# The channel mixer's depthwise taps read the gate from PSUM, and VectorE takes nearly all low parts of its weights

## The chip, the cores and the metric

The kernel runs on one core of one Trainium2 chip. The metric is the device time of one execution in microseconds (us). Ratios compare medians of runs taken side by side.

## The reference, cut to what matters

One layer of a diffusion backbone over 512 latent tokens of width 1024. After two token mixers comes the channel mixer, which is the part that is changed: a GEGLU network whose gate passes through a 3x3 depthwise convolution over the latent grid of 8 rows by 64 columns, with zeros outside the grid.

```python
def _conv_ffn(h, w_up, cw, cb, w_down, grid_h, grid_w):
    up = h @ w_up                                     # 1024 -> 2 x 2816
    g = _dwconv2d(up[..., :D_FF].reshape(B, grid_h, grid_w, D_FF), cw, cb).reshape(B, T, D_FF)
    return (jax.nn.gelu(g) * up[..., D_FF:]) @ w_down  # 2816 -> 1024
```

All of it is float32.

## The kernel before

**Products.** Every large product is made of three passes on TensorE. Each operand is split into a high part (`wh`, a cast) and a low part (`wl`, the operand less its high part), and `mm3` adds high x high, high x low and low x high in one PSUM bank. `Weights.prepare` (lines 85 to 97) makes the weights' parts block by block: a load into `raw` (two buffers), a cast to `wh` on ScalarE (line 93) and a subtraction to `wl` on VectorE or, for blocks marked `on_pool`, on GpSimd (line 95). `wh` and `wl` have three buffers each, so a block waits for the product three blocks earlier. `W.take` prepares two blocks ahead, with a raised priority.

**The channel mixer.** The 2816 gate channels and 2816 value channels are 22 tiles of 128 channels, in two stages: tiles 0 to 11, then 12 to 21. For each tile TensorE makes the gate `pg` and the value `pv`, one weight block and 24 matmuls of 512 columns each, into two of the six PSUM banks of the pool `ps`. Then `up_post` (lines 789 to 807) works on the tile: ScalarE copies the gate to a padded SBUF grid `gpad` (line 792, three buffers) and makes the centre tap with the bias in `acc` (line 794, two buffers); VectorE adds the eight other taps, each a multiply-add over a shifted window of the padded copy (line 797); ScalarE applies the GELU (line 800); VectorE multiplies with `pv` (line 802); ScalarE and VectorE split the result into `fh` and `fl` (lines 805, 806). After the tiles of a stage come its down products (`d`), in two halves with four PSUM tiles each. Tiles 0 and 1 are made with the halves of the second norm, and tiles 2 to 5 are each followed by the transposes of `token_major`.

**Order.** Each engine runs its instructions in an order that the tile planner fixes beforehand, from priorities and its own estimate of when each is ready. PSUM banks are handed out by the planner as well: a bank is free when the last reader of its tile is done. In the kernel before, the low parts of tile 0 and of all odd tiles are on GpSimd, the others on VectorE. The blocks of `w_down` are all on VectorE.

Of the kernel before, what the change touches and what calls it, by code (L numbers as in the profile page):

```python
# [10 lines left out]
F32 = mybir.dt.float32  # L11
F32R = mybir.dt.float32r
AF = mybir.ActivationFunctionType
ALU = mybir.AluOpType
PSUM = bass.MemoryType.PSUM

P = 128
# [11 lines left out]
GRID_W = 64  # L29
ROWS = T // GRID_W  # L30
# [77 lines left out]
def hybrid_block(ctx: ExitStack, tc: tile.TileContext, a: dict, out: bass.AP):  # L108
    nc = tc.nc

    def pool(name, bufs=1, side="left"):
        return tc.tile_pool(name=name, bufs=bufs, side=side, reuse_waits="tile")

    def opened(name, bufs=1, side="left"):
        stack = ExitStack()
        return stack, stack.enter_context(pool(name, bufs, side))
# [30 lines left out]
    def add_tiles(name, j, n=BLK, **kw):  # L147
        W.add(a[name][j], [n, n], **kw)
# [21 lines left out]
        add_tiles("w_out", i)  # L170
    for i0, i1 in STAGES:
        for i in range(i0, i1):
            add_tiles("w_up", i, on_pool=i == 0 or i % 2 == 1, extra=i == 0)
        for hf in range(2):
            for i in range(i0 // 2, i1 // 2):
                W.add(a["w_down"][hf, i], [BLK])
# [3 lines left out]
    def col(name, i, n=1):  # L180
        o = _cols[name] + i
        return sm[:, o : o + n]
# [190 lines left out]
    with pool("lamp") as lp:  # L373
# [3 lines left out]
        q = lp.tile([P, 20], F32, name="q")  # L377
# [21 lines left out]
    for i in range(2):  # L399
        t = lru.tile([P, PADW], F32, name=f"pad{i}")  # L400
# [199 lines left out]
    with pool("sp") as sp:  # L600
# [4 lines left out]
        for j in range(NG):  # L605
# [9 lines left out]
            for n in range(4):  # L615
                nc.vector.scalar_tensor_tensor(s[:, n, :], pz[:, n * P : (n + 1) * P], col("gv", j), bsb[:, j, :],
                                               op0=ALU.mult, op1=ALU.add)
# [158 lines left out]
            nc.scalar.copy(x1[:, t, hf * T : (hf + 1) * T], tp)  # L776


    GP = GRID_W + 2
    fp, f_pool = opened("f", side="right")  # L780
    fw = ctx.enter_context(pool("ffn"))
    gpads = []
    for i in range(3):
        t = fw.tile([P, ROWS + 2, GP], F32, name=f"gpad{i}")
        nc.gpsimd.memset(t, 0.0)
        gpads.append(t)
    fs = {}

    def up_post(i, pg, pv):
        pad = gpads[i % 3]  # L790
        g3 = pg.rearrange("p (r c) -> p r c", c=GRID_W)
        nc.scalar.copy(pad[:, 1 : 1 + ROWS, 1 : 1 + GRID_W], g3)
        acc = fw.tile([P, ROWS, GRID_W], F32, tag="acc", name=f"acc{i}", bufs=2)
        nc.scalar.activation(acc, g3, AF.Identity, scale=col("ffw", 9 * i + 4), bias=col("ffb", i))  # L794
        for q in (0, 1, 2, 3, 5, 6, 7, 8):
            dy, dx = q // 3, q % 3
            nc.vector.scalar_tensor_tensor(acc, pad[:, dy : dy + ROWS, dx : dx + GRID_W], col("ffw", 9 * i + q),  # L797
                                           acc, op0=ALU.mult, op1=ALU.add)
        accf = acc.rearrange("p r c -> p (r c)")
        nc.scalar.activation(accf, accf, AF.Gelu_apprx_tanh)  # L800
        f = fw.tile([P, T], F32, tag="f", name=f"f{i}", bufs=2)
        nc.vector.tensor_tensor(f, accf, pv, op=ALU.mult)
        fh = f_pool.tile([P, T], F32R, tag="fh", name=f"fh{i}", bufs=14)
        fl = f_pool.tile([P, T], F32R, tag="fl", name=f"fl{i}", bufs=14)
        nc.scalar.copy(fh, f)
        nc.vector.tensor_tensor(fl, f, fh.bitcast(F32), op=ALU.subtract)
        fs[i] = (fh, fl)
# [8 lines left out]
    for st, (i0, i1) in enumerate(STAGES):  # L816
        i = i0
        if st == 0:
            up_post(0, pu[0, 0], pu[0, 1])
            up_post(1, pu[1, 0], pu[1, 1])  # L820
            i = 2
        while i < i1:
            for s in range(2):
                pu[i, s] = mm_tile(f"up{i}{s}")
                gemm(pu[i, s], W.take(), h2h, h2l)
            up_post(i, pu[i, 0], pu[i, 1])
            if 2 <= i < 6:
                token_major(i - 2)
            i += 1
# [103 lines left out]
```

## Time and profile before

| What | Value |
|---|---|
| median of 3 runs (lowest to highest) | 991.13 us (991.07 to 996.96) |
| the profiled execution's own time | 989.86 us |
| its span, first to last instruction | 988.1 us |
| mean granted TensorE clock | 0.995 of full speed |
| PE (TensorE matmul) busy | 951.6 us |
| DVE (VectorE) busy | 665.2 us (67%) |
| ACT (ScalarE) busy | 478.0 us (48%) |
| POOL (GpSimd) busy | 95.0 us (10%) |
| chain that ended last | PE 65%, DVE 16%, ACT 8%, issue 6% |

Matmuls overlap their neighbours in the records, so the busy time of PE is longer than the time its stream needs; the distance between the starts of matmuls is the better measure. The channel mixer fills the span from about 604 us on.

### The profile page before, as it was taken

Reading aid. Unit: us, or ns where it says so; the run is one execution under the profiler, and the core shown is the slowest. Engines: PE = TensorE matmul, PEld = TensorE weight load, DVE = VectorE, ACT = ScalarE, POOL = GpSimd, SP = SyncE. Lnnn points to the kernel's source line nnn. Section 1 sums busy time; section 2 is a strip of 40 time slices with the busy share of each in tenths; the row PEclk is TensorE's granted clock in tenths of the full one; section 3 lists DMA queues with packets and bytes.
Section 4 is the critical chain, followed back from the end, with each engine's and each line's share of the span. In section 5 each row is a group of like instructions: output and inputs, shape, how many; then the busy total and the mean of one; then the engine's idle time right before and its main releaser. Section 6 shows DMA issues by size and latency. Waiting matters only on the chain.

```text
span 988.1 us, 11916 instructions
## 1 busy us (share of the span) xinstructions
PE 951.6 (96%) x4787; PEld 789.4 (80%) x4787; DVE 665.2 (67%) x867; ACT 478.0 (48%) x661; POOL 95.0 (10%) x92
## 2 busy tenths in 40 slices
PE   3999999999999999999999998999999999999997
PEld 2788888888888788788888798888778888887686
DVE  3768496968574976586634456798886447888764
ACT  4546979786989552234222343443333213333333
POOL 0000000000000011100001031222220002222020
PEclk9999999999999999999999999999999999999999
DMA  9532212132222276734524331222213332221232
GB/s 355 223 134 86 78 51 86 43 107 86 86 86 86 86 257 233 257 148 175 198 97 170 111 125 43 86 86 86 85 43 108 105 128 86 85 86 64 84 109 86
DMA packets 23511, 116.85 MB, mean 118 GB/s; under 512 B 2576, under 2 KB 3744, under 8 KB 14368
## 3 DMA queue, kind: packets, MB, share of 16 engines
q1 hardware_dynamic: 17488, 94.59, 26.9%
q0 software_dynamic: 5968, 21.50, 6.2%
q8 instruction: 37, 0.61, 0.2%
q14 instruction: 18, 0.15, 0.1%
HBM read 113.98 MB, written 2.10 MB: 117 GB/s over the span
## 4 chain that ended last, share of the span: by engine, by line
PE 65%; DVE 16%; ACT 8%; issue 6%; DMA 3%; POOL 1%; SPq 0%; ACTq 0%; DVEq 0%; POOLq 0%
DVE acc L797 8%; PE d L140 4%; PE d L141 4%; PE d L139 4%; PE up L139 4%; PE up L141 4%; PE up L140 4%; DVE wl L95 2%; DMA wmod<-in_w_mod 2%; ACT wh L93 2%; PE pg L139 2%; PE pg L140 2%; PE pg L141 2%; PE gg L141 1%; PE gg L140 1%
## 5 line engine op out<-in xcount | busy, mean ns | idle before, releaser
L93 ACT CAST wh<-raw 128x1024 fp32r<-128x1024 f32 (+1 forms) x156 | 161.3, 1038 | 231.6 <-PE d L141 44.6
L95 DVE TENSOR_TENSOR wl<-raw,wh 128x1024 fp32r<-128x1024 f32 (+1 forms) x132 | 159.4, 1210 | 119.9 <-ACT wh L93 119.3
L797 DVE SCALAR_TENSOR_TENSOR acc<-gpad,sm,acc 128x512 f32<-128x512 f32 x176 | 159.4, 916 | 19.1 <-ACT acc L794 15.0
L141 PE MATMUL up<-h2h,wl 128*128 128x512 f32 (+1 forms) x384 | 145.1, 378 | 6.8 <-POOL wl L95 6.8
L139 PE MATMUL up<-h2h,wh 128*128 128x512 f32 (+1 forms) x384 | 144.8, 377 | 1.4 <-ACT wh L93 1.4
L140 PE MATMUL up<-h2l,wh 128*128 128x512 f32 (+1 forms) x384 | 143.9, 375 | 0.0
L141 PEld LDWEIGHTS up<-h2h,wl 128*128 128x128 f32 x384 | 73.2, 191 | 23.3 <-POOL wl L95 8.8
L95 POOL TENSOR_TENSOR wl<-raw,wh 128x1024 fp32r<-128x1024 f32 x24 | 61.2, 2552 | 292.4 <-ACT wh L93 280.4
L139 PEld LDWEIGHTS up<-h2h,wh 128*128 128x128 f32 x384 | 73.1, 190 | 14.8 <-ACT wh L93 2.9
L140 PEld LDWEIGHTS up<-h2l,wh 128*128 128x128 f32 x384 | 73.3, 191 | 12.5
L800 ACT ACTIVATE acc<-acc 128x512 f32<-128x512 f32 x22 | 13.9, 632 | 134.5 <-DVE acc L797 134.5
L140 PE MATMUL d<-wl,fh 128*128 128x512 f32 (+1 forms) x186 | 72.0, 387 | 0.1
L141 PE MATMUL d<-wh,fl 128*128 128x512 f32 (+1 forms) x186 | 71.1, 382 | 0.0
L139 PE MATMUL d<-wh,fh 128*128 128x512 f32 (+1 forms) x186 | 71.0, 382 | 0.0
L558 DVE SCALAR_TENSOR_TENSOR wmod<-wmod,cbx 128x1024 f32<-128x1024 f32 x24 | 29.2, 1222 | 27.4 <-DMA wmod<-in_w_mod 27.3
L140 PEld LDWEIGHTS d<-wl,fh 128*128 128x128 f32 x186 | 34.9, 188 | 8.8 <-DVE wl L95 1.4
L139 PEld LDWEIGHTS d<-wh,fh 128*128 128x128 f32 x186 | 34.9, 188 | 7.9
L141 PEld LDWEIGHTS d<-wh,fl 128*128 128x128 f32 x186 | 35.0, 188 | 7.2
L555 POOL DMA_DIRECT2D wmod<-in_w_mod x32 | 16.9, 528 | 246.4 <-DVE yrl L538 128.8
L474 DVE TENSOR_TENSOR i<-i,xr 128x768 f32<-128x768 f32 x20 | 18.9, 954 | 19.7 <-ACT i L467 19.7
L140 PE MATMUL pr<-yrl,wh 128*128 128x512 f32 x80 | 31.7, 396 | 0.0
L141 PE MATMUL pr<-yrh,wl 128*128 128x512 f32 x80 | 31.7, 396 | 0.0
(316 smaller groups left out, 2162.1 us busy)
## 6 DMA issues: line engine op xcount, KB each, us to landing
raw<-in_w_up SPq DMA_DIRECT2D x22, 1024.0 KB, 4.7
wmod<-in_w_mod POOLq DMA_DIRECT2D x32, 512.0 KB, 4.1
raw<-in_w_down SPq DMA_DIRECT2D x22, 512.0 KB, 3.2
wm<-in_w_mod SPq DMA_DIRECT2D x8, 1024.0 KB, 8.8
raw<-in_w_lru SPq DMA_DIRECT2D x5, 1024.0 KB, 4.7
raw<-in_w_pr SPq DMA_DIRECT2D x5, 1024.0 KB, 6.4
raw<-in_w_rx SPq DMA_DIRECT2D x4, 1024.0 KB, 4.8
raw<-in_w_rg SPq DMA_DIRECT2D x4, 1024.0 KB, 4.7
```

Of the source, the lines that this page charges most:

```text
L93: nc.scalar.copy(h[:, :n], r)
L95: eng.tensor_tensor(l[:, :n], r, h[:, :n].bitcast(F32), op=ALU.subtract)
L139: nc.tensor.matmul(o, wh, xh, start=first, stop=False)
L140: nc.tensor.matmul(o, wh, xl, start=False, stop=False)
L141: nc.tensor.matmul(o, wl, xh, start=False, stop=last)
L474: nc.vector.tensor_tensor(i[u], i[u], xr[h][:, u % 2, :], op=ALU.mult)
L555: nc.gpsimd.dma_start(wm, a["w_mod25"][n - 2, k])
L558: nc.vector.scalar_tensor_tensor(wm, wm, 1.0, cbx, op0=ALU.mult, op1=ALU.mult, accum_out=m)
L797: nc.vector.scalar_tensor_tensor(acc, pad[:, dy : dy + ROWS, dx : dx + GRID_W], col("ffw", 9 * i + q), acc, op0=ALU.mult, op1=ALU.add)
L800: nc.scalar.activation(accf, accf, AF.Gelu_apprx_tanh)
```

## The change

The taps read the gate where TensorE left it, in PSUM. Each tap covers only the part of the grid for which its shifted source exists: 7 of 8 rows when it reaches up or down, 63 of 64 columns when it reaches left or right. The padded copies, their memsets and the ScalarE copy are removed. The low parts of `w_up` are all on VectorE, except those of tiles 0 and 1, which stay on GpSimd.

```diff
-            add_tiles("w_up", i, on_pool=i == 0 or i % 2 == 1, extra=i == 0)
+            add_tiles("w_up", i, on_pool=i <= 1, extra=i == 0)
...
-    gpads = []
-    for i in range(3):
-        t = fw.tile([P, ROWS + 2, GP], F32, name=f"gpad{i}")
-        nc.gpsimd.memset(t, 0.0)
-        gpads.append(t)
...
-        pad = gpads[i % 3]
         g3 = pg.rearrange("p (r c) -> p r c", c=GRID_W)
-        nc.scalar.copy(pad[:, 1 : 1 + ROWS, 1 : 1 + GRID_W], g3)
         acc = fw.tile([P, ROWS, GRID_W], F32, tag="acc", name=f"acc{i}", bufs=2)
         nc.scalar.activation(acc, g3, AF.Identity, scale=col("ffw", 9 * i + 4), bias=col("ffb", i))
         for q in (0, 1, 2, 3, 5, 6, 7, 8):
-            dy, dx = q // 3, q % 3
-            nc.vector.scalar_tensor_tensor(acc, pad[:, dy : dy + ROWS, dx : dx + GRID_W], col("ffw", 9 * i + q),
-                                           acc, op0=ALU.mult, op1=ALU.add)
+            dy, dx = q // 3 - 1, q % 3 - 1
+            r0, r1 = max(0, -dy), ROWS - max(0, dy)
+            c0, c1 = max(0, -dx), GRID_W - max(0, dx)
+            o = acc[:, r0:r1, c0:c1]
+            nc.vector.scalar_tensor_tensor(o, g3[:, r0 + dy : r1 + dy, c0 + dx : c1 + dx], col("ffw", 9 * i + q), o,
+                                           op0=ALU.mult, op1=ALU.add)
```

## Rows read from the trace of the kernel before

**Rows 1.** The page, part 1: busy time, share of the span, instructions.
```profile
PE 951.6 (96%) x4787; PEld 789.4 (80%) x4787; DVE 665.2 (67%) x867; ACT 478.0 (48%) x661; POOL 95.0 (10%) x92
```
**Rows 2.** Waits of PE in the up products: total us, times, longest.
```profile
PE up L141 <- POOL wl L95: 6.8, 4, 1.7
...
PE up L139 <- ACT wh L93: 1.4, 3, 0.5
```
**Rows 3.** Windows: length, busy (count) per engine, granted clock, DMA share, GB/s.
```profile
622.00:686.00 64.00, 64.00 (x302) 53.37 (x301) 56.65 (x66) 32.09 (x47) 15.33 (x6) 1.00 0.24 82
686.00:734.00 48.00, 45.36 (x194) 35.35 (x193) 39.15 (x44) 15.33 (x22) 8.42 (x5) 1.00 0.23 77
734.00:743.00 9.00, 7.30 (x24) 5.52 (x25) 7.83 (x9) 1.86 (x3) 2.20 (x1) 0.81 0.22 64
743.00:812.00 69.00, 69.00 (x297) 55.53 (x296) 34.03 (x42) 18.00 (x20) 0.40 (x1) 1.00 0.35 122
812.00:890.00 78.00, 78.00 (x345) 64.61 (x345) 62.01 (x66) 25.63 (x35) 17.49 (x7) 1.00 0.24 81
890.00:924.00 34.00, 30.13 (x128) 23.34 (x128) 26.81 (x31) 12.26 (x17) 7.52 (x3) 1.00 0.18 62
924.00:946.00 22.00, 21.90 (x93) 16.79 (x92) 15.51 (x19) 8.25 (x11) 0.00 (x0) 1.00 0.34 103
```
**Rows 4.** Timeline of DVE, end of stage one: start us, us, what.
```profile
722.50 8.28 DVE L797 SCALAR_TENSOR_TENSOR acc<-gpad,sm,acc 128x512 f32<-128x512 f32 x8
...
734.96 5.72 DVE L797 SCALAR_TENSOR_TENSOR acc<-gpad,sm,acc 128x512 f32<-128x512 f32 x6 [1.42 <-ACT acc L794]
...
746.30 1.23 DVE L95 TENSOR_TENSOR wl<-raw,wh 128x1024 fp32r<-128x1024 f32 x1 [0.26 <-ACT wh L93]
747.46 4.69 DVE L797 SCALAR_TENSOR_TENSOR acc<-gpad,sm,acc 128x512 f32<-128x512 f32 x6
752.06 1.22 DVE L95 TENSOR_TENSOR wl<-raw,wh 128x1024 fp32r<-128x1024 f32 x1
753.20 1.53 DVE L797 SCALAR_TENSOR_TENSOR acc<-gpad,sm,acc 128x512 f32<-128x512 f32 x2
```
**Rows 5.** Timeline of ACT, the same stretch.
```profile
743.30 0.63 ACT L800 ACTIVATE acc<-acc 128x512 f32<-128x512 f32 x1 [7.44 <-DVE acc L797]
...
745.22 1.05 ACT L93 CAST wh<-raw 128x1024 fp32r<-128x1024 f32 x1
746.17 0.58 ACT L792 COPY gpad<-up 128x512 f32<-128x512 f32 x1
746.64 0.78 ACT L794 ACTIVATE acc<-up,sm 128x512 f32<-128x512 f32 x1
...
754.77 0.63 ACT L800 ACTIVATE acc<-acc 128x512 f32<-128x512 f32 x1 [6.41 <-DVE acc L797]
```
**Rows 6.** The line of the taps: shortest, median, longest ns, first and last start.
```profile
L797 DVE SCALAR_TENSOR_TENSOR acc<-gpad,sm,acc x176: 736/752/2896, 625.4 to 936.9; 128x512 f32<-128x512 f32 x176
```
**Rows 7.** Lines by form: xcount, busy us, mean ns, idle before, releaser.
```profile
L797 DVE SCALAR_TENSOR_TENSOR acc<-gpad,sm,acc 128x512 f32<-128x512 f32 x176 | 159.4, 916 | 19.1 <-ACT acc L794 15.0
...
L673 DVE SCALAR_TENSOR_TENSOR x1c<-o,mcol,x1c 128x512 f32<-128x512 f32 x5 | 3.8, 751 | 14.7 <-PE o L141 14.7
L673 DVE SCALAR_TENSOR_TENSOR x1c<-o,mcol,x1c 128x256 f32<-128x256 f32 x6 | 2.9, 476 | 2.3 <-PE o L141 2.3
```
**Rows 8.** The page, part 6: weight loads, KB each, us to landing.
```profile
raw<-in_w_up SPq DMA_DIRECT2D x22, 1024.0 KB, 4.7
```
**Rows 9.** Timelines of DVE, PE and ACT at the first tiles.
```profile
625.39 12.74 DVE L797 SCALAR_TENSOR_TENSOR acc<-gpad,sm,acc 128x512 f32<-128x512 f32 x14 [0.96 <-ACT acc L794]
...
634.05 0.48 PE L139 MATMUL up<-h2h,wh 128*128 128x512 f32 x1
...
638.16 0.63 ACT L800 ACTIVATE acc<-acc 128x512 f32<-128x512 f32 x1 [1.61 <-DVE acc L797]
```

More of the change, by code (lines that the diff above doesn't have):

```diff
@@ L776, in token_major @@
             nc.scalar.copy(x1[:, t, hf * T : (hf + 1) * T], tp)
-    GP = GRID_W + 2
     fp, f_pool = opened("f", side="right")
     fw = ctx.enter_context(pool("ffn"))
-    gpads = []
-    for i in range(3):
-        t = fw.tile([P, ROWS + 2, GP], F32, name=f"gpad{i}")
-        nc.gpsimd.memset(t, 0.0)
-        gpads.append(t)
     fs = {}
     def up_post(i, pg, pv):
-        pad = gpads[i % 3]
         g3 = pg.rearrange("p (r c) -> p r c", c=GRID_W)
-        nc.scalar.copy(pad[:, 1 : 1 + ROWS, 1 : 1 + GRID_W], g3)
         acc = fw.tile([P, ROWS, GRID_W], F32, tag="acc", name=f"acc{i}", bufs=2)
```

## The prediction

> **What bounds the kernel now.** I began with the busy times on the page: PE is busy for 96% of the span [rows 1], which says that only what shortens PE's stream or its gaps can shorten the run. The list of PE's waits names 8.2 us in the up products, most of it for low parts from GpSimd [rows 2]. That is too little, since overlapping matmuls hide the start of a gap, so I counted matmuls per window instead [rows 3]. From 812 to 890 us PE starts 345 in 78 us, 0.226 us apart; that is its pace when nothing is late, and a tile (48 matmuls) then takes 10.85 us. At that pace the other windows of the up products need 194 x 0.226 = 43.9 of 48 us, 24 x 0.226 = 5.4 of 9, and 128 x 0.226 = 28.9 of 34: 4.1, 3.6 and 5.1 us are lost. The down products run 0.232 apart (297 in 69 us), so 924 to 946 loses 22 - 93 x 0.232 = 0.4. The sum is **13.2 us**. Part of the 3.6 is TensorE at the lower of its levels for a while: the window's granted clock is 0.81, after PE had waited.
>
> Why only there? The timelines show that the work behind the products goes round in a loop, one turn per tile: GELU, product with the value, `fh`, next `wh`, its `wl`, taps, GELU. The taps of three tiles running start at 722.50, 734.96 and 747.46 [rows 4], 12.5 us apart, which is 1.65 more than PE's 10.85. So PE's lead over that loop shrinks by 1.65 us per tile. In stage two it lasts from 812 to 890 us, 7 tiles, or some 11.6 us of lead; then PE waits for weight parts at each turn.
>
> **The loop without GpSimd** is already in the trace. Behind the last tile of each stage come blocks of `w_down`, whose low parts are all VectorE's. The GELUs at 743.30 and 754.77 enclose such a turn: 11.47 us [rows 5], although VectorE makes two low parts in it [rows 4]. The six taps from 747.46 take 4.69 us there, but 5.72 from 734.96, when GpSimd works, and eight take 8.28 from 722.50. The line's median tap is 752 ns, its longest 2896 [rows 6], its mean 916 [rows 7]: taps that meet GpSimd wait for it. That is 176 x 0.164 = 28.9 us of VectorE, against 20 x 1.14 us (752.06 to 753.20) = 22.8 us for the 20 low parts that are moved.
>
> **The change, part by part.**
>
> *Low parts moved.* The loop becomes the one of 11.47 us for every tile: 1.0 us less. Behind a low part that waits for `wh` stand the taps on VectorE, and behind those the GELU; the 11.47 includes both. GpSimd's queue loses work and nobody else waits for it. The raw buffer of an odd tile comes free later, as its second low part now stands behind six taps; the load lands in 4.7 us [rows 8] and has more than a turn, so nothing.
>
> *Smaller taps.* Four corners of 7 x 63, two of 7 x 64, two of 8 x 63: 458.5 elements on average, not 512. The nearest row with a PSUM source is the same operation at line 673: 751 ns for 512 elements and 476 for 256 [rows 7], 1.07 ns per element. So a tap is 752 - 53.5 x 1.07 = 695 ns, 0.46 us less per tile: a loop of **11.0 us**. Bounds: 476 ns below, 916 above (a tap as slow as today's mean). I take 695, since line 673 reads PSUM while PE writes other banks and is no slower than a padded tap.
>
> [...]
>
> *The copy removed.* It takes 0.5 us of ScalarE at 746.17, but `acc` ends at 747.42 and `wl` at 747.53 [rows 4, 5]: the low part releases the taps just as late. Nothing inside the loop; about 0.5 us at a stage's first taps. The memsets sit on an idle GpSimd: nothing.
>
> *PE's lead.* 11.0 against 10.85 costs 0.15 us of lead per tile, 1.5 per stage, out of 11.6. The lead is no longer used up, and of the 13.2 us lost I take all back but 0.2. If the lower clock of 734 to 743 came from elsewhere, up to 1.6 us of it would stay (the 9 us at 0.81 are worth 7.3 at full clock).
>
> *Banks held longer.* The gate's bank came free after `acc`; now it is held to the last tap. In the regular part this costs nothing: tile i+3 takes tile i's banks 32.6 us after tile i began, and the taps are done by then. At the first tiles it does. Tiles 0, 1 and 2 fill all six banks, and tile 3 begins at 634.05 [rows 9]. Taps of tiles 0 and 1 are interleaved: 14 run from 625.39, and the GELU of tile 0 waits for the last of them, until 638.16 [rows 9]. Afterwards, 14 x 0.71 (with the gap between two) = 9.9 us, and one of tile 3's low parts among them 1.1 (the other fits where the copies were): bank free at 636.5, so PE waits **2.5 us**, and no later slack takes it back. Bounds: 0, if tile 0's taps all go first (625.4 + 5.7 + 1.1 = 632.2), and 5.0, if all 16 taps and both low parts do (639.1).
>
> **Sum.** 989.9 - 13.2 + 0.2 + 2.5 = 979.4 on the profiled execution's own time (989.86, 1.8 above its span). The median of the runs is 991.13, 1.3 higher: **980.5 us** to the half. Its own range is 976 to 984: no wait for a bank below (978), a wait of 5.0 and a leftover clock dip above.
>
> **Rivals.**
>
> *The waits only change hands* (0.20). Every odd tile's second low part goes behind six taps, where GpSimd made it at once. If the planner puts it later, behind all eight, or orders the weight casts anew, PE waits for VectorE instead. For it: orders are fixed beforehand and will be made anew. Against it: even tiles have had this order all along, and the 812 to 890 window, which holds such tiles, loses nothing. It leaves about the 8.2 us of recorded waits in place: 980.5 + 8.2, so 985 to 990.
>
> *Taps from PSUM cost more* (0.08). The lead of 11.6 us over 10 tiles allows a loop of 12.0, so taps up to 0.695 + 1.0 / 8 = 0.82 us; beyond that each further 0.1 us per tap costs 0.8 us per late tile. At 916 ns the loop is 12.8 and all is lost: 982 to 992. For it speaks only that no row has eight reads of one bank in a row, in pieces of rows; against it, line 673 [rows 7]. [...]
>
> *Banks starve PE all through* (0.12), the slower side. If taps of two tiles are interleaved not only at the start but all through stage one, each pair holds both gates to the end, and PE waits at each of six pairs for up to the 5.0 us above: 989.9 - 13.2 + 30 = 1006.7, so 1002 to 1008 on the median. It decides when a tile's last tap comes over 32.6 us after its gate's first product. For it: the banks are just enough for three tiles. Against it: in the regular part six and two, or eight, taps of one tile follow each other [rows 4].
>
> **Chances.** My forecast has 0.60, the rivals 0.20, 0.08 and 0.12. The range of 8 in 10 is 976 to 990: the forecast, the first rival and most of the second. About 1% (9.9 us, to 981.2) is what a measurement here can tell from no change, and the forecast lies just beyond it: of its 0.60, some 0.10 falls short. So faster 0.50, same 0.10 + 0.20 + 0.08 = 0.38, slower 0.12.
>
> **What would show it.** The GELUs of a stage should stand 10.9 to 11.1 us apart, not 12.5. Taps should take 0.67 to 0.75 us, with none above 1 us once tile 1's low parts are made. PE should start its up products 0.226 to 0.23 us apart through both stages, with no wait at line 141 for a low part. It should wait once, near 634 us, for a VectorE tap. Taps of 0.8 us and more, a chain of waits for `wl` on VectorE, or a wait for banks at every second tile would prove me wrong, each for its rival. The down products and the tail should take as long as before.

## The result, and the profile after

The changed kernel takes **977.5 us** (median of 4 runs, 975.9 to 979.2). The kernel before, run beside it on the same chip, takes 993.0 (4 runs, 991.1 to 997.0). The ratio is 0.985, with an interval of 0.983 to 0.988: 1.5% faster. The profiled execution of the changed kernel took 978.6 us with a span of 976.8; before it was 989.9 and 988.1.

The first lines to read are the busy times and the shares of the chain that ended last, from the page of the changed kernel.

```profile
PE 947.4 (97%) x4787; PEld 790.9 (81%) x4787; DVE 645.4 (66%) x887; ACT 469.6 (48%) x639; POOL 41.6 (4%) x69
...
PE 78%; issue 6%; DVE 6%; ACT 6%; DMA 3%; POOL 1%; SPq 0%; POOLq 0%; DVEq 0%; ACTq 0%
```

The chain ran through PE for 65% of the span and through DVE for 16%; now it is 78% and 6%. PE's busy time hardly moves (951.6 to 947.4), although the span is 11 us shorter. Busy time counts an instruction from its start to its modelled end, so a busy PE can hide late starts. DVE makes 20 more instructions than before and is busy 20 us less [rows 1].

Counting the matmuls says more. These are windows of the changed kernel: length, then busy time and count per engine (PE, PEld, DVE, ACT, POOL), then granted clock, DMA share and GB/s.

```profile
622.00:686.00 64.00, 64.00 (x313) 53.87 (x312) 55.87 (x78) 29.20 (x40) 0.00 (x0) 1.00 0.28 99
686.00:734.00 48.00, 48.00 (x213) 39.75 (x213) 39.39 (x53) 18.11 (x24) 0.00 (x0) 1.00 0.23 77
734.00:743.00 9.00, 9.00 (x41) 7.33 (x40) 8.00 (x12) 2.19 (x3) 0.00 (x0) 1.00 0.36 117
812.00:890.00 78.00, 78.00 (x346) 64.58 (x345) 65.02 (x86) 27.68 (x36) 0.00 (x0) 1.00 0.27 95
890.00:924.00 34.00, 34.00 (x150) 27.94 (x149) 26.84 (x36) 11.14 (x14) 0.00 (x0) 1.00 0.27 87
...
625.30:737.70 112.40, 112.40 (x514) 93.39 (x513) 98.75 (x135) 46.91 (x63) 0.00 (x0) 1.00 0.27 94
804.90:913.80 108.90, 108.90 (x482) 90.10 (x482) 88.74 (x117) 38.27 (x49) 0.00 (x0) 1.00 0.26 91
913.79:969.88 56.09, 56.09 (x271) 46.51 (x269) 28.41 (x42) 19.15 (x33) 6.32 (x4) 1.00 0.22 76
```

Set the first five against [rows 3]. In 686 to 734 PE starts 213 matmuls where it started 194; 890 to 924 has 150 for 128. The pace of 812 to 890, 0.226 us per matmul, now holds in the other windows of up products too (48 / 213 and 34 / 150 are 0.225 and 0.227), and the granted clock is 1.00 in all of them. The last three windows are the up products of the two stages and the last down products, by their own beginnings and ends. The same stretches of the kernel before, which begin and end elsewhere in time, are these three.

```profile
622.35:743.00 120.65, 116.31 (x514) 93.90 (x513) 103.62 (x118) 49.06 (x71) 25.95 (x10) 0.99 0.23 79
810.20:924.30 114.10, 110.23 (x481) 89.65 (x480) 90.70 (x98) 38.95 (x53) 25.41 (x10) 1.00 0.22 78
924.31:981.15 56.84, 56.74 (x271) 46.18 (x269) 35.80 (x51) 22.31 (x38) 6.45 (x4) 1.00 0.28 93
```

The up products of stage one take 112.4 us instead of 120.65 (514 matmuls in both), those of stage two 108.9 instead of 114.1, and the last down products 56.1 instead of 56.8: **8.25 + 5.2 + 0.75 = 14.2 us** taken back. The down products of stage one take 67.2 in both (737.7 to 804.9 now, 743.0 to 810.2 before). The span fell by 11.3 only, since the work ahead of these stages ended 2.9 us later in this execution (the first product of tile 2 starts at 625.26, before at 622.35). That is not the change: a transfer of `wmod` came late there (VectorE waits 3.88 us for it, until 429.86). In the same kernel profiled again the point is 622.40, and over all ten profiled executions of the experiments below it lies anywhere from 622.4 to 626.0.

Where the taps stand is seen in their line, all 176 of them (shortest, median, longest ns), and in the groups by form, which end in mean ns and the idle time ahead.

```profile
L793 DVE SCALAR_TENSOR_TENSOR acc<-up,sm,acc x176: 662/677/744, 625.2 to 917.4; 128x441 f32<-128x441 f32 x88, 128x448 f32<-128x448 f32 x44, 128x504 f32<-128x504 f32 x44
```
```profile
L793 DVE SCALAR_TENSOR_TENSOR acc<-up,sm,acc 128x441 f32<-128x441 f32 x88 | 58.7, 672 | 12.1 <-ACT acc L786 10.7
...
L793 DVE SCALAR_TENSOR_TENSOR acc<-up,sm,acc 128x504 f32<-128x504 f32 x44 | 32.6, 740 | 1.2
...
L793 DVE SCALAR_TENSOR_TENSOR acc<-up,sm,acc 128x448 f32<-128x448 f32 x44 | 30.0, 682 | 1.2
```

No tap waits any more: the longest takes 744 ns, where it was 2896 [rows 6], and the mean is 121.3 us / 176 = 689 instead of 916 [rows 7].

ScalarE's timeline near the end of stage one shows who leads now (start, duration, what, and the idle time ahead with what ended it).

```profile
698.61 0.63 ACT L796 ACTIVATE acc<-acc 128x512 f32<-128x512 f32 x1 [3.37 <-DVE acc L793]
...
705.07 1.05 ACT L93 CAST wh<-raw 128x1024 fp32r<-128x1024 f32 x1 [3.19 <-PE up L140]
709.49 0.63 ACT L796 ACTIVATE acc<-acc 128x512 f32<-128x512 f32 x1 [3.37 <-DVE acc L793]
```

The GELUs stand 10.88 us apart, and the casts between them wait for PE to free a `wh`. The turn is now as long as PE's 48 matmuls; the loop follows PE, no longer PE the loop. In PE's list of waits no up product appears.

### The profile page after: what moved, and what is told of

Same layout as the page of the kernel before. It is cut to its first block, busy times and chain, and to the rows that moved or that the text cites. A ratio compares the mean times of both kernels' runs of the same rounds, so it can differ in the third digit from the quotient of the medians.

```text
span 976.8 us, 11886 instructions
## 1 busy us (share of the span) xinstructions
PE 947.4 (97%) x4787; PEld 790.9 (81%) x4787; DVE 645.4 (66%) x887; ACT 469.6 (48%) x639; POOL 41.6 (4%) x69
## 4 chain that ended last, share of the span: by engine, by line
PE 78%; issue 6%; DVE 6%; ACT 6%; DMA 3%; POOL 1%; SPq 0%; POOLq 0%; DVEq 0%; ACTq 0%
PE up L139 8%; PE up L140 8%; PE up L141 8%; PE d L140 4%; PE d L139 4%; PE d L141 4%; DMA wmod<-in_w_mod 2%; PE pg L139 2%; PE pg L140 2%; PE pg L141 2%; PE gg L140 1%; PE gg L141 1%; PE gg L139 1%; PE g L141 1%; PE g L140 1%
## 5 line engine op out<-in xcount | busy, mean ns | idle before, releaser
L95 DVE TENSOR_TENSOR wl<-raw,wh 128x1024 fp32r<-128x1024 f32 (+1 forms) x152 | 183.9, 1212 | 143.8 <-ACT wh L93 142.4
L793 DVE SCALAR_TENSOR_TENSOR acc<-up,sm,acc 128x441 f32<-128x441 f32 (+2 forms) x176 | 120.1, 692 | 14.5 <-ACT acc L786 10.7
L141 PEld LDWEIGHTS up<-h2h,wl 128*128 128x128 f32 x384 | 72.9, 190 | 12.5
L474 DVE TENSOR_TENSOR i<-i,xr 128x768 f32<-128x768 f32 x20 | 18.9, 953 | 19.8 <-ACT i L467 19.8
L139 PE MATMUL pr<-yrh,wh 128*128 128x512 f32 x80 | 31.7, 396 | 0.0
L140 PE MATMUL g<-xrl,wh 128*128 128x512 f32 x80 | 31.7, 396 | 0.0
```

The costliest lines, as they stand in the source:

```text
L95: eng.tensor_tensor(l[:, :n], r, h[:, :n].bitcast(F32), op=ALU.subtract)
L139: nc.tensor.matmul(o, wh, xh, start=first, stop=False)
L140: nc.tensor.matmul(o, wh, xl, start=False, stop=False)
L141: nc.tensor.matmul(o, wl, xh, start=False, stop=last)
L474: nc.vector.tensor_tensor(i[u], i[u], xr[h][:, u % 2, :], op=ALU.mult)
L793: nc.vector.scalar_tensor_tensor(o, g3[:, r0 + dy : r1 + dy, c0 + dx : c1 + dx], col("ffw", 9 * i + q), o, op0=ALU.mult, op1=ALU.add)
```

## The experiments

All times are medians. Each run was compared with the kernel before on its own chip, so kernels from two chips are best compared by their ratios. The kernel before took 990.8 us beside the first four, 992.2 beside the two with SBUF taps next to GpSimd's low parts and with six more operations, and 990.9 beside the other four. Theory A is the one that I held when the run was put on record. It is that of the prediction, except in three runs. For the changed taps alone the prediction's account, in which the moved low parts end the waiting, is nearer to theory B. For the SBUF taps beside GpSimd and for the six more operations, A was made anew from the runs ahead of them.

**The changed kernel again,** with no edit.

> The changed kernel again, as the measure for the other three on this chip. Theory (the loop behind the products falls below PE's 10.85 us per tile): ratio 0.984 to 0.988 to the kernel before; GELUs 10.9 us apart in both stages. The profiled execution of the changed kernel lost 2.9 us ahead of the channel mixer, where a modulation row's transfer came late; if that is chance, here the first up product of tile 2 starts within 1 us of 622.4, as before the change.

977.4 us (975.8 to 981.2), ratio 0.987 [0.983, 0.990]. Up products 112.5 us in stage one (622.40 to 734.89) and 108.8 in stage two (802.09 to 910.93). This is the reference for what follows.

**The taps changed, the low parts as before.** In the changed kernel:

```diff
-            add_tiles("w_up", i, on_pool=i <= 1, extra=i == 0)
+            add_tiles("w_up", i, on_pool=i == 0 or i % 2 == 1, extra=i == 0)
```

> Only the taps change: read from PSUM on part of the grid, no copy; the odd tiles' low parts stay on GpSimd. Theory A (a tap with one SBUF input does not wait for GpSimd, so the 28.9 us of waiting go as well): taps all under 0.8 us, the loop has one low part less on VectorE than the changed kernel's and stays under 10.85 us, PE loses nothing; ratio 0.984 to 0.988, the same as the whole change. Theory B (the move of the low parts is what frees the loop): taps still reach 2 us and more beside GpSimd, the loop is 12.5 - 0.46 = 12.0 us, about 1.2 us per tile of lead are used up, PE loses some 2 to 6 us; ratio 0.989 to 0.995.

977.1 us, ratio 0.986 [0.983, 0.990]: the whole gain, although GpSimd makes its 20 low parts again. VectorE's timeline and GpSimd's, of one stretch:

```profile
853.72 5.09 DVE L793 SCALAR_TENSOR_TENSOR acc<-up,sm,acc 128x441 f32<-128x441 f32 x7 [1.73 <-ACT acc L786]
...
865.12 5.81 DVE L793 SCALAR_TENSOR_TENSOR acc<-up,sm,acc 128x441 f32<-128x441 f32 x8
```
```profile
853.08 2.40 POOL L95 TENSOR_TENSOR wl<-raw,wh 128x1024 fp32r<-128x1024 f32 x1 [3.00 <-ACT wh L93]
869.45 2.40 POOL L95 TENSOR_TENSOR wl<-raw,wh 128x1024 fp32r<-128x1024 f32 x1 [13.96 <-ACT wh L93]
```

Both groups of taps overlap a low part of GpSimd, and a tap in them takes 0.73 us (5.09 / 7 and 5.81 / 8), as in the changed kernel, where five without GpSimd take 3.66 (at 702.46). The longest of all 176 takes 745 ns. A tap that reads one input from PSUM did not wait for GpSimd here.

**The low parts changed, the taps as before.** In the kernel before:

```diff
-            add_tiles("w_up", i, on_pool=i == 0 or i % 2 == 1, extra=i == 0)
+            add_tiles("w_up", i, on_pool=i <= 1, extra=i == 0)
```

> Only the low parts move to VectorE; padded copies and full taps as before. Theory A (what counts is the lead: 11.47 us per tile use up 0.62 x 10 = 6.2 of 11.6 us): PE loses nothing in either stage, ratio 0.984 to 0.988, the same as the whole change. Theory B (the loop itself sets the pace): GELUs and products 11.47 us apart, 20 x 0.62 = 12.4 us of the gain lost, ratio 0.996 to 1.000.

978.0 us, ratio 0.986 [0.983, 0.989]: again the whole gain, with the padded copy and 512 elements per tap. Its taps are down to a mean of 751 ns, with GpSimd off them:

```profile
L797 DVE SCALAR_TENSOR_TENSOR acc<-gpad,sm,acc 128x512 f32<-128x512 f32 x176 | 130.0, 751 | 3.8
```

The turn wasn't the 11.47 us that I had read from [rows 5]. ScalarE's timeline, and the taps of VectorE:

```profile
699.03 0.63 ACT L800 ACTIVATE acc<-acc 128x512 f32<-128x512 f32 x1 [4.09 <-DVE acc L797]
699.57 1.03 ACT L93 CAST wh<-raw 128x1024 fp32r<-128x1024 f32 x1
700.51 0.62 ACT L805 CAST fh<-f 128x512 fp32r<-128x512 f32 x1
...
709.69 0.63 ACT L800 ACTIVATE acc<-acc 128x512 f32<-128x512 f32 x1 [3.87 <-DVE acc L797]
...
720.36 0.63 ACT L800 ACTIVATE acc<-acc 128x512 f32<-128x512 f32 x1 [3.65 <-DVE acc L797]
```
```profile
702.38 3.90 DVE L797 SCALAR_TENSOR_TENSOR acc<-gpad,sm,acc 128x512 f32<-128x512 f32 x5
```

The GELUs are 10.66 to 10.67 apart: shorter than PE's turn, with taps of full size. That lasts until 720 us; from there they follow PE, 10.88 apart. The planner made a new order. The `wh` cast now goes ahead of `fh`, and its low part ahead of `fl`, so that ScalarE's casts no longer stand one behind the other on VectorE's path. From the GELU to the taps behind it is 3.35 us (699.03 to 702.38), where it was 4.16 in the turn of the prediction (743.30 to 747.46 [rows 4, 5]): that is the whole difference of 0.81. A's result held, but not its length of the loop.

**Taps from an unpadded copy in SBUF,** low parts as changed. In the changed kernel:

```diff
+        gs = fw.tile([P, ROWS, GRID_W], F32, tag="gs", name=f"gs{i}", bufs=3)
+        nc.scalar.copy(gs, g3)
...
-            nc.vector.scalar_tensor_tensor(o, g3[:, r0 + dy : r1 + dy, c0 + dx : c1 + dx], col("ffw", 9 * i + q), o,
+            nc.vector.scalar_tensor_tensor(o, gs[:, r0 + dy : r1 + dy, c0 + dx : c1 + dx], col("ffw", 9 * i + q), o,
```

> The changed kernel with the gate copied to an unpadded SBUF tile by ScalarE, the same partial taps reading the copy. Theory A (a PSUM source costs VectorE no more than an SBUF source; line 673): taps of 672, 682 and 740 ns by shape, as from PSUM, ratio as the changed kernel's within 0.002. [...]

977.0 us, ratio 0.985 [0.982, 0.988]. The copy costs nothing, and the taps by form are these:

```profile
L795 DVE SCALAR_TENSOR_TENSOR acc<-gs,sm,acc 128x441 f32<-128x441 f32 x88 | 59.0, 676 | 1.5
...
L795 DVE SCALAR_TENSOR_TENSOR acc<-gs,sm,acc 128x504 f32<-128x504 f32 x44 | 32.2, 743 | 1.2
...
L795 DVE SCALAR_TENSOR_TENSOR acc<-gs,sm,acc 128x448 f32<-128x448 f32 x44 | 29.8, 683 | 1.0
```

676, 743 and 683 ns from SBUF, 672, 740 and 682 from PSUM: no difference that matters. The GELUs of stage two stand 11.08 us apart here, 0.2 more than PE's turn, and PE loses nothing (112.5 and 108.8 us): over ten tiles that takes 2 us of PE's lead.

**The same with GpSimd's low parts back.** In that last kernel the `on_pool` line of the first edit was put back. It differs from the kernel with the changed taps alone only in where the taps read, and in the copy that this needs.

> Partial taps from the unpadded SBUF copy, and the odd tiles' low parts on GpSimd: the taps-only kernel with an SBUF source, nothing else. Theory A (what the change took away is taps waiting for GpSimd, in an order that was fixed without knowing of those waits): the longest taps take 2 us and more again, GELUs stand about 12.0 us apart (12.5 less 0.46 for the size), PE loses 1 to 6 us of its stream in the two stages, against none in the taps-only kernel. Theory B (size of taps and work on VectorE count, the source doesn't): GELUs 10.9 us apart, no loss, the same time as the taps-only kernel.

986.1 us (984.7 to 987.9), ratio 0.994 [0.992, 0.996]: 6 us faster than the kernel before, and by the ratios (0.994 against 0.986) some 7 slower than with PSUM taps; the medians, from two chips, are 9 apart. The line of the taps, VectorE's timeline, GpSimd's, and PE's wait:

```profile
L795 DVE SCALAR_TENSOR_TENSOR acc<-gs,sm,acc 128x441 f32<-128x441 f32 x88 | 85.7, 977 | 15.3 <-ACT acc L788 13.7
```
```profile
853.23 7.83 DVE L795 SCALAR_TENSOR_TENSOR acc<-gs,sm,acc 128x441 f32<-128x441 f32 x8
...
865.31 6.19 DVE L795 SCALAR_TENSOR_TENSOR acc<-gs,sm,acc 128x441 f32<-128x441 f32 x7 [1.42 <-ACT acc L788]
```
```profile
854.22 2.67 POOL L95 TENSOR_TENSOR wl<-raw,wh 128x1024 fp32r<-128x1024 f32 x1 [11.86 <-ACT wh L93]
...
864.19 2.41 POOL L95 TENSOR_TENSOR wl<-raw,wh 128x1024 fp32r<-128x1024 f32 x1 [7.31 <-ACT wh L93]
```
```profile
PE up L141 <- POOL wl L95: 4.6, 3, 1.5
```

Eight taps beside a low part now take 7.83 us instead of 5.81; the seven that begin in the middle of one take 6.19 instead of 5.09. The longest single tap is 2854 ns. The GELUs are 12.1 us apart (836.92, 849.08, 861.16, 873.32). So the four cells of source and engine are filled: taps with both inputs in SBUF **and** low parts on GpSimd give the long turn; taking away either ends it. The copy is too small to be the cause: it takes 0.58 us of ScalarE, while the taps wait for 2.0 us (7.83 - 5.81) and 1.1 us (6.19 - 5.09) in alternate turns.

Beside GpSimd's low parts the longest tap is thus 2854 ns with two SBUF inputs and 745 ns with one. What holds such a tap up inside the chip, the runs don't show.

**Tile 0's bank held longer.** Eight more reads of its gate in the changed kernel, into a scratch tile; nothing else uses them.

```diff
+        for _ in range(8 if i == 0 else 0):
+            extra = fw.tile([P, ROWS, GRID_W], F32, tag="extra", name=f"extra{i}", bufs=1)
+            nc.vector.scalar_tensor_tensor(extra, g3, col("ffw", 9 * i), acc, op0=ALU.mult, op1=ALU.add)
```

> The changed kernel with eight more reads of tile 0's gate in PSUM by VectorE (results unused), which hold its bank and delay the work of tiles 0 and 1 by some 5 to 6 us. Theory A (the bank term was real, and only its size was off: in the changed kernel the bank comes free some 0.6 us ahead of need): PE now waits 2 to 5 us once, near the first product of tile 3, for VectorE, and nothing later gives it back: 2 to 5 us above the changed kernel. Theory B (banks never bind, or a later slack absorbs it): no wait, the time of the changed kernel within 1 us.

979.1 us, ratio 0.987 [0.984, 0.991]. The up products of stage one take 115.0 us (622.71 to 737.72), 2.5 more than in the unedited kernel. PE's timeline at tile 3, and VectorE's:

```profile
633.62 1.04 PE L775 MATMUL tq<-ident,x1c 128*128 128x128 f32 x8
...
639.68 0.50 PE L139 MATMUL up<-h2h,wh 128*128 128x512 f32 x1 [0.70 <-DVE acc L793]
```
```profile
638.96 0.66 DVE L793 SCALAR_TENSOR_TENSOR acc<-up,sm,acc 128x441 f32<-128x441 f32 x1
639.55 3.88 DVE L797 SCALAR_TENSOR_TENSOR extra<-up,sm,acc 128x512 f32<-128x512 f32 x5
```

PE waits for a tap before tile 3's first product, and the planner put transposes of later work into part of the hole, which then wait for their own copies (0.9 us in three waits). The tap is the last one of tile 1, at 638.96. Tile 0's own reads run on to 643.4, so the bank that tile 3 took here is that of tile 1, whose taps three of the extra reads had delayed. The loss is never given back. The medians don't show it (a ratio of 0.987 with and without the edit); the stage's length does.

**The same at tile 8,** in the middle of the stage: `8 if i == 8 else 0`.

> The same eight reads, at tile 8, in the middle of stage one. Theory A (PE has a lead of some 11 us there, and a bank is wanted only 32.6 us after its tile began): no wait of PE, the time of the changed kernel within 1 us. Theory B (PE is tied to the loop at every tile): 5 to 6 us above it.

976.2 us, ratio 0.985 [0.981, 0.989]; stage one 112.5 us (622.94 to 735.42). No wait of PE is recorded in the stage. The last extra read begins at 717.17, and tile 11, three tiles on, starts at 724.53: nothing wanted the bank while it was held. So a bank held longer cost something at the first tiles, where all six are full and PE wants one at once, and nothing here.

**More work for VectorE at each tile,** one, three and six multiply-adds of 512 elements (1, 3 or 6 in the range), each reading `acc` alone, into a scratch tile. They stand between the taps and the GELU.

```diff
+        extra = fw.tile([P, ROWS, GRID_W], F32, tag="extra", name=f"extra{i}", bufs=1)
+        for _ in range(3):
+            nc.vector.scalar_tensor_tensor(extra, acc, col("ffw", 9 * i), acc, op0=ALU.mult, op1=ALU.add)
```

> The changed kernel with one more multiply-add of 512 elements per tile on VectorE (reads acc twice, result unused): the loop goes from 11.0 to 11.8 us. Theory A (lead of 11.6 us, 0.95 x 10 = 9.5 used up per stage): nothing or nearly, 0 to 2 us above the changed kernel. Theory B (the loop sets the pace as soon as it is longer than PE's 10.85 us): 20 x 0.8 = 16 us above.

> Three more per tile: the loop goes to 13.3 us. Theory A (lead gone after 11.6 / 2.45 = 4.7 tiles, then 2.45 us lost per tile in the remaining 5 of each stage): 20 to 30 us above the changed kernel, ratio 1.005 to 1.016 to the kernel before. Theory B (VectorE is 66% busy and PE 97%, so 50 us more of VectorE hide): within 2 us of the changed kernel.

> The changed kernel with six more multiply-adds of 512 elements per tile on VectorE (results unused). With three more VectorE was busy for 75.4 of 78 us and nothing was lost. Theory A (the bound behind PE is VectorE's whole work per tile, not the turn of a fixed order): 10.5 + 3 x 0.66 = 12.5 us per tile against 10.85, GELUs 12.5 us apart on average, PE loses 1.65 us per tile once a lead of some 11 us per stage is used up: 5 to 15 us above the changed kernel. Theory B (the planner hides this as well): within 2 us of it.

One more: 977.8 us, ratio 0.986 [0.983, 0.989], no loss. Three more: 978.1 us, ratio 0.986 [0.983, 0.990], no loss either, where 20 to 30 us were expected by A. Six more: 1008.7 us, ratio 1.017 [1.015, 1.020], some 30 us behind the changed kernel by the ratios, where 5 to 15 were expected. With three more, a window of stage two reads:

```profile
830.00:908.00 78.00, 78.00 (x346) 64.59 (x345) 75.40 (x106) 27.97 (x35) 0.00 (x0) 1.00 0.24 85
```

VectorE is busy for 75.4 of 78 us, and PE still starts its 346. The timeline of VectorE there shows why a fixed loop doesn't describe this.

```profile
846.06 0.74 DVE L797 SCALAR_TENSOR_TENSOR extra<-acc,sm 128x512 f32<-128x512 f32 x1
846.72 0.67 DVE L793 SCALAR_TENSOR_TENSOR acc<-up,sm,acc 128x441 f32<-128x441 f32 x1
847.31 0.74 DVE L797 SCALAR_TENSOR_TENSOR extra<-acc,sm 128x512 f32<-128x512 f32 x1
...
848.75 0.69 DVE L801 TENSOR_TENSOR f<-acc,up 128x512 f32<-128x512 f32 x1
```

The planner put the next tile's taps between the extra reads of this one, and ahead of and behind the product with the value: VectorE no longer idles while ScalarE makes the GELU. With 75.4 / 78 of PE's 10.88 us per tile, VectorE has 10.5 us of work. Three more (some 2 us) make 12.5, over PE's 10.88. With six more, VectorE is busy for 127 of the 132.5 us of stage one (its window is shown first), so that no order could help much. PE's list of waits follows:

```profile
623.13:755.61 132.48, 119.61 (x514) 96.40 (x513) 127.01 (x183) 44.42 (x59) 0.00 (x0) 0.96 0.23 80
```
```profile
PE up L139 <- DVE f L801: 11.5, 4, 4.2
...
PE up L139 <- DVE acc L793: 5.0, 3, 3.4
PE d L139 <- ACT acc L799: 3.3, 2, 1.7
```

The waits of the up products all stand at the first matmul of a gate or of a value, so they are for banks. Stage one is 20.0 us longer (132.5), stage two 6.1 (114.95), the down products behind them 1.9 and 2.0. Stage two loses about what A gives for a stage, 10 x (12.5 - 10.85) - 11 = 5.5; stage one loses far more. Whether it had less lead or lost more behind each wait (see the last section), these runs don't separate.

## Why the prediction was right, point by point

**What bounds the kernel: right.** PE loses time in the up products nearly alone, and a loop that meets GpSimd is the cause. Counting matmuls gave 13.2 us, and 14.2 came back; PE's list of waits had only 8.2.

**Low parts moved: right, and enough by itself** (978.0). I had the loop at 11.47 for this part. It was 10.66 while it ran ahead of PE, because the planner's order is made anew with each edit. The raw buffer and GpSimd's queue cost nothing, as said.

**Smaller taps: right in size, no part of the time.** 689 ns measured, 695 worked out. But with the low parts moved, taps of 751 ns reach the same end. They count only where GpSimd stays in the loop: with SBUF taps beside GpSimd's low parts the kernel takes 986.1 against 992.2 before, and the turn is 12.1 instead of 12.5 us.

**PSUM as a source: right that it costs no more.** What the prediction read from line 673 holds for the taps: 672 ns from PSUM and 676 from SBUF at 441 elements. What the prediction missed is what the source does besides: it takes the taps out of GpSimd's way (the longest is 745 ns where it is 2854 from SBUF). I costed the new source only by its duration, and credited the end of the waiting to the moved low parts alone. Either part would have done it, and the two gains are one.

**The copy removed: right,** nothing (977.0 with a copy).

**PE's lead: the result right, the model wrong.** The GELUs came 10.88 apart, in the range of 10.9 to 11.1 but for 0.02, and nothing of the loss stayed. Yet a loop of fixed length that eats 11.6 us of lead is no general description. By it, three extra operations would cost 20 to 30 us and cost none; turns of 12.1 us would use up the lead only at the stage's end, yet with SBUF taps beside GpSimd PE lost 5.0 us in stage one (117.55 against 112.5) and 2.3 in stage two. That a lead exists is borne out: turns of 11.08 us cost nothing. What held in these runs: an order in which VectorE doesn't idle keeps up to about 10.5 us of its work per tile.

**Banks held longer: the one mis-sized term,** 2.5 us forecast, 0 measured. It was within its bounds, but not for the reason given there: the taps of tiles 0 and 1 stayed interleaved. The timelines of ScalarE, VectorE and PE at the first tiles, to set against [rows 9]:

```profile
624.39 0.78 ACT L786 ACTIVATE acc<-up,sm 128x512 f32<-128x512 f32 x1 [10.39 <-PE up L141]
625.07 1.99 ACT L93 CAST wh<-raw 128x1024 fp32r<-128x1024 f32 x2
```
```profile
628.78 3.14 DVE L793 SCALAR_TENSOR_TENSOR acc<-up,sm,acc 128x441 f32<-128x441 f32 x5
...
632.98 3.73 DVE L793 SCALAR_TENSOR_TENSOR acc<-up,sm,acc 128x441 f32<-128x441 f32 x6
```
```profile
636.97 0.48 PE L139 MATMUL up<-h2h,wh 128*128 128x512 f32 x1
```

Tile 0's centre tap is planned ahead of two `wh` casts that stood ahead of it before. Its first tap begins 0.1 us ahead of tile 2's first product (625.20 against 625.26), where it began 3.0 behind (625.39 against 622.35). And the interleaved taps follow each other by 0.62 us (3.73 / 6), not by 0.71. There are 13 of them here and not 14. Three low parts stand among them, where I had counted one, which takes back some 2.3, and the taps of tile 0 end by 636.71, just ahead of the product at 636.97. The margin is below 1 us. The edit that held tile 0's bank shows that such a wait can come there and that it isn't given back: 2.5 us, in that run for tile 1's bank.

**The sum.** 979.4 was forecast on the profiled execution's own time, and 978.6 came, but partly by two errors that cancel: the bank's 2.5, the lead's 0.2 and 1.0 more of gain make 3.7 us too many, and the late start of 2.9, which has nothing to do with the change, was on the other side. To that extent the 0.8 us between them is luck. In the medians 980.5 was forecast and 977.5 measured, while the kernel before took 993.0 beside it and not the 991.13 that the forecast started from. By the ratio (0.9852 of 991.13 is 976.5) the forecast was 4.0 us too high, most of it the bank.

**The rivals.** Waits that change hands to VectorE, dearer taps from PSUM, and banks that starve PE all through the stage: none came. The second and the third could be provoked, by other means: SBUF taps beside GpSimd give 986.1 us, six extra operations give bank waits and 1008.7.

**No version beat the changed kernel** by more than the scatter of the runs. It, the two halves of the change and the taps from a copy lie within 977.0 to 978.0 us, and PE starts its matmuls 0.226 us apart through both stages.

## What to carry to other kernels

Count an engine's starts per window against its best stretch; the busy share and the list of waits both hid a part of this loss. Where VectorE and GpSimd work at the same time, look at the longest instance of an operation beside its median: if an operation with two SBUF inputs waits (2854 ns here, 745 with one input in PSUM), move one input to PSUM or the work off GpSimd, and expect the gain once. A turn read from a trace is the planner's order for that kernel and not a constant of the work; compare the engine's whole work per tile with the bound, and look separately at the first tiles, where the buffers are all full.

## What the runs showed of the hardware that was not expected

- Multiply-adds that write different tiles follow each other sooner: in the timeline of three more, the next one starts 0.59 us behind one of 0.67, and 0.66 behind one of 0.74. Taps on one accumulator stand 0.73 apart, and the five extra reads in a row at 639.55, which don't need each other's result but write one tile, (3.88 - 0.75) / 4 = 0.78. An order that interleaves two tiles gains some 0.1 us per tap here (0.62 against 0.73).
- Reading PSUM for eight taps in pieces of rows is as fast as reading SBUF (672 against 676 ns for 441 elements), while PE writes other banks (a matmul each 0.226 us).
- GpSimd's low part also takes longer when it begins while SBUF taps run: 2.67 us at 854.22 and 2.68 at 878.45. Where it began ahead of the taps it took 2.41 (at 864.19). Beside PSUM taps the four from 847.68 to 874.84 take 2.40 to 2.41; over all 24 the mean is 2495 ns with SBUF taps and 2432 with PSUM taps.
- With six more, PE waits 4.21 us for a bank, until 748.44. From 748.4 to 752.0 the granted clock is then 0.56, and the matmuls that start at 749.59, 750.02 and 750.45 stand 0.43 apart instead of 0.226. From 752 to 758 it is 0.98 again. The same spacing follows the waits that end at 669.78, 707.63 and 932.48 (3.4, 2.8 and 4.2 us). Part of the loss of a wait thus comes behind it: in that run's stages 30.0 us were lost (20.0 + 6.1 + 1.9 + 2.0), of which the waits named above are 19.8. In the kernel before, the granted clock is 0.50 from 737 to 740, with matmuls at 737.04, 737.46 and 737.89, behind a wait of 1.70 us that ends at 736.25, and 1.00 from 740 to 743; behind a wait of 1.70 us that ends at 711.29 it is 1.00 (711 to 716).
